# One layer with two recurrent mixers and a ConvFFN: two additions of the out-projection stage made by accumulating GpSimd transfers, and a new order of all engines

## The chip, the cores and the metric

The kernel runs on one core of a Trainium2 chip. The metric is the time on the device, in microseconds (us), of one execution, from its start to its end. A core has five engines that run side by side, each with its own queue of instructions: TensorE (PE in the profile, its weight loads PEld), VectorE (DVE), ScalarE (ACT), GpSimd (POOL) and SyncE (SP). Transfers between the core's memory and the chip's main memory are issued by SP or by GpSimd and carried out by 16 DMA engines.

## The reference

One layer, 1024 wide, works on 1152 tokens: 1024 latent tokens and 128 context tokens. Two mixers share one input projection; each runs over the tokens in both directions. Their outputs are added, normalised, projected and added to the input (the residual), and a gated feed-forward network with a 3x3 convolution follows. Cut to what matters here:

```python
h = rmsnorm(x, norm_mix_w) * (1 + scale1) + shift1
u = h @ w_in
o_a = rmsnorm(o_f + flip(o_b), hgrn_norm_w) * silu(g)          # HGRN2, chunks of 64 tokens
y = y_f + flip(y_b)                                            # RWKV-7: the two directions
yn = (y - mean(y)) * rsqrt(var(y) + GN_EPS) * ln_w + ln_b      # per head of 64
o_b = (yn + bonus) * g
x = x + gate1 * (concat([o_a, o_b]) @ w_out)                   # residual
h = rmsnorm(x, norm_ffn_w) * (1 + scale2) + shift2
gt = dwconv(h @ ffn_w_gate) + ffn_conv_b
x = x + gate2 * ((gelu(gt) * (h @ ffn_w_up)) @ ffn_w_down)
```

All is float32. The outputs are the normed x of latent and context tokens and the mixers' new states.

## The kernel before, in words

The tokens lie in nine row tiles of 128 rows: tiles 0 to 7 are latent, tile 8 is the context. A float32 matrix product is made of three float32r matmuls: each operand is split into a rounded high part and a low rest (`split`), and hi·hi, lo·hi and hi·lo are added in PSUM.

**How the order comes about.** The kernel's code issues nothing itself. It records every operation with its tiles in a `Plan`, and `schedule()` then places the operations one by one on the engines, by a model of their durations: on each engine the ready operation of the highest rank comes next. The rank is the length of the work that hangs on the operation, plus a lead from two tables: `LEADS` by the piece of code that recorded it, and `NUDGE` by the operation's number divided by 16. `BUSY` is a bonus for dense matmuls where PE has been used little in the model's last stretch. `issue()` emits the order so found, with its waits. A change of the recorded operations or of these numbers can thus move instructions anywhere on any engine. `ld` is a load issued by SP; `st` is a store that goes to POOL or SP, whichever the plan finds better; `combine` is a VectorE operation on two tensors. Where a program's name ends in a number (`wh_131`), the number is a buffer's.

**The stages.** Up to about 490 us the input is normed, modulated and projected (L1125 to L1127, three matmuls of 128x384 a step). From about 486 to 973 us the RWKV chains run in 18 steps of 64 tokens for two groups of heads, with the HGRN2 blocks, the adaLN rows (L1032 to L1038) and the rest of the projections between them. L1302 is a transpose on PE that feeds from the copy L1298. In a chain step, L1631, L1646, L1776, L1820, L1827, L1846 and L1848 are small matmuls on PE. L1767 copies values, some of them on GpSimd. L1776 reads a tile that was loaded from `d_ak`. A step's outputs are written to the array `yd` in main memory, one half of it for each direction (L1875).

As soon as the rows of a tile are complete, `wo_tile(i)` handles the out-projection of that tile, in the order 3, 4, 8, 2, 5, 1, 6, and last 0 and 7 together. Its steps:

- `post` loads both directions of y (L1915, 512 KB) and the bonus and gate rows (L1916), adds the directions (L1921, VectorE, 128x512), norms y by heads (up to L1931), and transposes it (L1935).
- 48 matmuls with the out-projection's weights follow (L2011 to L2013), and VectorE multiplies their result by the gate (L2015).
- x is loaded (L2003, 512 KB), and added as the residual (L2017, VectorE, 128x1024). The sum is stored to `x2d` (L2018), since the FFN's end needs it again.
- The root mean square is worked out (L1134 to L1137); L2019 on ScalarE normalises, L2025 transposes on PE, L1991 scales and shifts on ScalarE or VectorE, and L2034 stores the result, save for the last two tiles.

From about 1033 us on the FFN runs: L2120 multiplies by the gate and up weights, in a scheme of partial products: the "a" ones of 320 columns (operand `qm`), then the "b" ones of 256 columns (operands `ham` and `hbm`, which are made of the last tiles' result by L2057 and L2053). The down projection (L2269 to L2271) and a last norm end the kernel.

Of the kernel before, what the change touches and what calls it, by code (L numbers as in the profile page):

```python
# [18 lines left out]
MUL, ADD, SUB = ALU.mult, ALU.add, ALU.subtract  # L19
# [24 lines left out]
FETCH = 42.0  # L44
AHEAD = 240.0
HUNGRY = 2.04
BUSY = 168.59
NUDGE = {1: 6, 3: -7, 4: -41, 5: -2, 7: 9, 8: 9, 9: 9, 10: 9, 11: 20, 12: 19, 13: 19, 14: 15, 15: 15, 16: 5, 17: -4, 18: -1, 19: -4, 20: -18, 21: -29, 22: -19, 23: -26, 24: -26, 25: -6, 27: -3, 28: -3, 29: -3, 30: -3, 31: -5, 32: -3, 33: -3, 35: -3, 51: -5, 52: -5, 53: -2, 84: -6, 85: -6, 86: -6, 87: -6, 88: 6, 91: -3, 92: -6, 93: -6, 94: -6, 95: -6, 96: -6, 97: -6, 98: -6, 104: -7, 105: -4, 108: -6, 109: 4, 110: -6, 111: -6, 119: 6, 127: -7, 140: 6, 141: 6, 142: 6, 143: 21, 144: 6, 145: 6, 147: -2, 172: -17, 173: -17, 174: -17, 175: -17, 183: -14, 184: -20, 185: -4, 189: 57, 190: 57, 191: 69, 193: 5, 194: 3, 200: -15, 201: -8, 203: 11, 204: 14, 206: 3, 212: -16, 217: 13, 218: 5, 224: -48, 225: -15, 226: -15, 227: -15, 236: 7, 239: -2, 243: -26, 244: -26, 245: -26, 246: -19, 247: -26, 251: 7, 252: 7, 253: 5, 254: -12, 266: -4, 269: 3, 275: 61, 282: -16, 290: -9, 292: 2, 294: 18, 295: 18, 296: 18, 297: 28, 298: 28, 299: 28, 300: 48, 301: 48, 302: 30, 303: 27, 305: 30, 306: 30, 307: 30, 308: 37, 309: 40, 310: 40, 311: 40, 312: 51, 313: 42, 314: 47, 315: 43, 316: 23, 317: 26, 318: 26, 319: 23, 320: 23, 321: 23, 322: 23, 323: 22, 328: 10, 329: 13, 330: 29, 331: 29, 337: -10, 338: -10, 339: -10, 340: -10, 341: -10, 342: -10, 343: -10, 344: 10, 345: 10, 346: 5, 347: 8, 348: 8, 349: 8, 350: 11, 351: 8, 352: -12, 353: -14, 354: -8, 355: -14, 356: 15, 357: -2, 358: 33, 359: 7, 360: -4, 361: 4, 362: -3, 363: -4, 364: 7, 365: -7, 367: 13, 368: 23, 370: 25, 377: 6, 378: 13, 379: 13, 380: 18, 381: 18, 382: 18, 390: 1, 396: 6, 398: 5, 400: -10, 401: -10, 404: -6, 405: -6, 406: -6, 407: -6, 408: -6, 409: -6, 410: -6, 411: -6, 412: -6, 413: -2, 416: -23, 417: 3, 418: 3, 419: 3, 425: -3, 426: -3, 427: -3, 428: -3, 453: -3, 454: -3, 455: -5, 456: 20, 457: 5, 458: 20, 459: 3, 460: -15, 461: 1, 462: -4, 463: -11, 464: -4, 465: -4, 466: -4, 467: -4, 468: -4, 469: -2, 470: 32, 471: 15, 472: 15, 473: 16, 474: 1, 475: 1, 476: 15, 477: 10, 478: 14, 479: 15, 480: 28, 481: 10, 482: 12, 483: 34, 484: 24, 485: 26, 486: 6, 487: 21, 488: 6, 489: 11, 490: 20, 491: 13, 492: 25, 493: 2, 494: -16, 495: -5, 496: -5, 497: -5, 498: -5, 499: -43, 500: -20, 501: -18, 502: -16, 503: -39, 504: -13, 505: -12, 506: -12, 507: -15, 508: -36, 509: -37, 510: -24, 511: -24, 512: -38, 516: 21, 517: 22, 518: 22, 519: 11, 520: 11, 521: 11, 522: 1, 523: 11, 524: 1, 525: 11, 526: 9, 527: 26, 528: -1, 529: 1, 530: -5, 532: -34, 533: -34, 534: -26, 535: -27, 536: 8, 537: 22, 538: 22, 539: 45, 540: 16, 541: 18, 542: 14, 543: 14, 544: 4, 545: 13, 546: 4, 547: 4, 548: 53, 549: 39, 550: 39, 551: 52}
LEADS = {'ada_block': 46.4, 'bonus_rows': 27.8, 'chains': -35.7, 'const': 113.0, 'conv_rkv': 0.0, 'down_weights': -36.2, 'elim': -4.6, 'features': 0.0, 'ffn_down': 14.5, 'ffn_mid': -1.7, 'finish': 52.5, 'finish_last': -12.3, 'first_columns': -38.6, 'front': 0.0, 'gate_row': 0.0, 'hgrn_block': -3.6, 'hgrn_in': 0.0, 'hgrn_out': 113.5, 'late': -0.7, 'made': 3.5, 'mod_columns': -1.2, 'mod_scale': 70.4, 'modulated': -24.2, 'pair': 8.2, 'param_loads': 9.6, 'params': -96.8, 'post': 3.0, 'prep': 119.5, 'product': -3.4, 'put': 0.0, 'save': 4.8, 'step_kernel': -1.0, 'stored': 0.0, 'three': -10.1, 'total': -0.3, 'turned': 4.0, 'weights': 0.0, 'wo_tile': 5.1}


C_W0, C_A0, C_KK, C_KA, C_RK, C_LNW, C_LNB = 0, 8, 12, 16, 20, 24, 28
# [125 lines left out]
class Plan:  # L178


    PIECES = ("proj", "small_proj", "norm_rows", "modulate", "gate_rows", "load_step", "load_values", "conv_tiles")
    HELPERS = ("mm", "st", "copy", "combine", "split", "load_w", "record", "either")
    ENGINES = ("PE", "DVE", "ACT", "POOL", "SP")
    BITS = 23
    ROW = 1 << 16
# [94 lines left out]
    @staticmethod  # L280
    def operands(m, args, kw):

        isap = lambda x: isinstance(x, AP)
        w = [args[0]]
        r = [x for x in args[1:] if isap(x)]
        for k, x in kw.items():
            if isap(x):
                (w if k == "accum_out" else r).append(x)
        if (m == "matmul" and not kw.get("start", True)) or m == "copy_predicated":
            r.append(args[0])  # L290
        return w, r

# [526 lines left out]
def step_kernel(ctx: ExitStack, tc: tile.TileContext, I, O):  # L819
    cp = ctx.enter_context(tc.tile_pool(name="cp", bufs=1, side="left", reuse_waits="tile"))  # L820
    plan = Plan(tc, cp.tile([P, 1], F32, name="base"))
    act, dve, pool, pe = (plan.engine(e) for e in ("ACT", "DVE", "POOL", "PE"))
    ld = plan.engine("SP").dma_start

    def st(out, src):

# [1084 lines left out]
    def post(i, oh, ol, early):  # L1911

        r = slice(i * P, (i + 1) * P)
        yt, vg = (tl(t + "10"[early], [P, 2, 512]) for t in ("py", "pvg"))
        ld(yt, yd[r])  # L1915
        ld(vg, vbd[i])  # L1916
        y, sq = yt[:, 0], yt[:, 1]
        hd = heads_of
        small = tl("sm" if early else "sm1", [P, 4, 8])
        each = lambda j: view(small, 8 * j, [[1, 8], [0, 64]])  # L1920
        combine(y, y, sq, ADD)  # L1921
        dve.tensor_reduce(small[:, 0], hd(y), mybir.AxisListType.X, ADD)
        dve.tensor_scalar(small[:, 0], small[:, 0], -1.0 / 64, None, MUL)
        combine(hd(y), hd(y), each(0), ADD)
        act.activation(sq, y, AF.Square)
        dve.tensor_reduce(small[:, 1], hd(sq), mybir.AxisListType.X, ADD)
        act.activation(small[:, 2], small[:, 1], AF.Sqrt, scale=1.0 / 64, bias=eps[:, 2:3])
        dve.reciprocal(small[:, 3], small[:, 2])
        combine(hd(y), hd(y), each(3), MUL)
        combine(y, y, vg[:, 1], MUL)  # L1930
        combine(y, y, vg[:, 0], ADD)  # L1931
        ps = pbank("a")
        with plan.together():
            for p in range(NPAIR):
                pe.transpose(ps[:, p * P:(p + 1) * P], y[:, p * P:(p + 1) * P], ident)  # L1935
        split(oh[:, 4:8], ol[:, 4:8], ps.rearrange("p (k t) -> p k t", k=4))
# [58 lines left out]
    def wo_tile(i, early):  # L1995

        raw = tl("wr", [P, 4, P])
        ld(raw, odram.rearrange("k p t -> p k t")[:, :, i * P:(i + 1) * P])
        oh, ol = tl("wh", [P, KT, P], F32R), tl("wl", [P, KT, P], F32R)
        split(oh[:, 0:4], ol[:, 0:4], raw)  # L2000
        post(i, oh, ol, early)
        x, x2 = tl("xw" if early else "xr", [P, 1024]), tl("x2w" if early else "x2", [P, 1024])
        ld(x, x_src(i))  # L2003
        g1 = gate1[:, i // 8 * 1024:(i // 8 + 1) * 1024]
        for n in range(2):
            nc_ = slice(n * 512, (n + 1) * 512)
            ps = pbank()
            for kt in range(KT):
                woh, wol = wo[kt, n]
                with plan.together():  # L2010
                    mm(ps, oh[:, kt, :], woh, kt == 0, False)  # L2011
                    mm(ps, oh[:, kt, :], wol, False, False)  # L2012
                    mm(ps, ol[:, kt, :], woh, False, kt == KT - 1)  # L2013
                plan.follow("dense")
            dve.tensor_tensor(x2[:, nc_], ps, g1[:, nc_], MUL)  # L2015
            yield
        combine(x2, x2, x, ADD)  # L2017
        st(x2d[i], x2)  # L2018
        act.activation(x, x2, AF.Identity, scale=norm_rows(x2, x, "nssw" if early else "nss2"))  # L2019
        t = x2.rearrange("p (k t) -> p k t", k=KT)  # L2020
        for k0 in (0, 4):
            ps = pbank("a")
            with plan.behind(scaled), plan.together():
                for kt in range(k0, k0 + 4):
                    pe.transpose(ps[:, (kt - k0) * P:(kt - k0 + 1) * P], x[:, kt * P:(kt + 1) * P], ident)  # L2025
            for kt in range(k0, k0 + 4):
                modulate(t[:, kt, :], ps[:, (kt - k0) * P:(kt - k0 + 1) * P], kt, i // 8,
                         ("ACT", "DVE") if i in (0, 7) else ("ACT",))
        yield t
# [366 lines left out]
```

## Time and profile before

| | |
|---|---|
| median of 3 runs | 1820.85 us (1820.06 to 1825.13) |
| the profiled execution's own time | 1820.69 us |
| its span, first to last instruction | 1818.9 us |
| mean granted TensorE clock | 0.993 |
| PE busy, of the span | 97% |
| VectorE, ScalarE, GpSimd busy | 78%, 47%, 16% |

A line of the profile names the engine, the line of the code, the operation, and the tiles that it writes and reads (`out<-in`, the tile's pool, such as `low` or `top`, where no name is its own). A wait is put down to the operation that came last of those that the instruction waited for. The granted clock is TensorE's, as a share of full speed. The DMA share is the mean busy share of the 16 DMA engines.

### The profile page before, as it was taken

The numbers are of one execution on the slowest core, as the hardware profiler recorded it, in microseconds if no ns is written. First come the engines' busy times: TensorE is split into PE (matmuls) and PEld (weight loads), VectorE is DVE, ScalarE is ACT, GpSimd is POOL, SyncE is SP. The second block draws the span as 40 slices with busy tenths as digits, with TensorE's granted clock in tenths as the row PEclk, the third lists the DMA queues.
The fourth block names the chain that finished last, engine by engine and source line by source line (L and its number), as shares of the span: only waits on it lengthen the run. The fifth ranks groups of instructions, "written<-read, shape, count | busy, mean of one in ns | idle before, by whom it ended". The sixth has DMA issues, their size and how long they took to land.

```text
span 1818.9 us, 45180 instructions
## 1 busy us (share of the span) xinstructions
PE 1768.3 (97%) x18402; PEld 1587.1 (87%) x18402; DVE 1415.1 (78%) x2670; ACT 862.0 (47%) x1753; POOL 289.3 (16%) x553
## 2 busy tenths in 40 slices
PE   7999999999999999999999999999999999999998
PEld 5889888899888788888788799999999999888887
DVE  7559899887778888876867889999999954985543
ACT  6556656543255645643636754444444433321321
POOL 2013435353312222122110100000000000000000
PEclk9999999999999999999999999999999999999999
DMA  9325637487757568889967522222222247774451
GB/s 325 102 72 151 147 102 180 128 229 193 207 165 246 165 203 258 267 283 306 324 207 244 203 59 73 73 73 73 73 73 73 76 126 251 227 272 162 133 169 67
DMA packets 272176, 307.45 MB, mean 169 GB/s; under 512 B 62611, under 2 KB 216849, under 8 KB 271968
## 3 DMA queue, kind: packets, MB, share of 16 engines
q1 hardware_dynamic: 245584, 224.33, 41.3%
q0 software_dynamic: 26384, 80.23, 13.1%
q8 instruction: 144, 2.36, 0.5%
q14 instruction: 64, 0.52, 0.1%
HBM read 200.50 MB, written 103.99 MB: 167 GB/s over the span
## 4 chain that ended last, share of the span: by engine, by line
PE 69%; DMA 5%; DVE 3%; ACT 1%; issue 1%; POOL 0%; SPq 0%; DVEq 0%; ACTq 0%; POOLq 0%
PE banks L2120 27%; PE banks L2269 5%; PE banks L2270 5%; PE banks L2271 5%; PE banks L1125 3%; PE banks L1127 3%; PE banks L1126 3%; DMA low<-d_ak 2%; PE banks L2011 2%; PE banks L2013 2%; PE banks L2012 2%; PE banks L1776 1%; PE banks L1827 1%; PE banks L1846 1%; PE banks L1646 1%
## 5 line engine op out<-in xcount | busy, mean ns | idle before, releaser
L1125 PE MATMUL banks<-hh,wh 128*128 128x384 f32 x768 | 282.0, 367 | 0.7 <-DVE fx L1314 0.7
L1127 PE MATMUL banks<-hh,wl 128*128 128x384 f32 x768 | 259.0, 337 | 0.0
L1126 PE MATMUL banks<-hl,wh 128*128 128x384 f32 x768 | 258.7, 337 | 0.0
L2209 DVE SCALAR_TENSOR_TENSOR low<-low,pf 128x1024 f32<-128x1024 f32 x176 | 224.8, 1279 | 4.6 <-ACT low L2203 3.0
L2120 PE MATMUL banks<-qm,wh 128*128 128x320 f32 x968 | 223.3, 310 | 0.0
L2120 PE MATMUL banks<-hbm,wh 128*128 128x256 f32 x880 | 164.4, 283 | 1.3 <-ACT low L1991 1.3
L1125 PEld LDWEIGHTS banks<-hh,wh 128*128 128x128 f32 x768 | 144.9, 189 | 21.0 <-issue 11.4
L2120 PE MATMUL banks<-qm,wl 128*128 128x320 f32 x528 | 162.8, 308 | 0.0
L2120 PEld LDWEIGHTS banks<-qm,wh 128*128 128x128 f32 x968 | 160.7, 189 | 0.1
L1126 PEld LDWEIGHTS banks<-hl,wh 128*128 128x128 f32 x768 | 145.5, 189 | 2.4 <-issue 1.2
L1127 PEld LDWEIGHTS banks<-hh,wl 128*128 128x128 f32 x768 | 145.0, 189 | 0.0
L2120 PEld LDWEIGHTS banks<-hbm,wh 128*128 128x128 f32 x880 | 140.4, 191 | 1.7 <-ACT low L1991 1.7
L2120 PE MATMUL banks<-ham,wh 128*128 128x256 f32 (+1 forms) x616 | 132.4, 295 | 0.0
L2120 PE MATMUL banks<-hbm,wl 128*128 128x256 f32 x440 | 124.8, 284 | 0.0
L2120 PEld LDWEIGHTS banks<-ham,wh 128*128 128x128 f32 x616 | 102.2, 192 | 0.0
L2120 PEld LDWEIGHTS banks<-qm,wl 128*128 128x128 f32 x528 | 99.1, 188 | 0.0
L2269 PE MATMUL banks<-qm,hbm 128*128 128x512 f32 (+1 forms) x240 | 93.7, 390 | 0.0
L2270 PE MATMUL banks<-qm,hbm 128*128 128x512 f32 (+1 forms) x240 | 93.6, 390 | 0.0
L2271 PE MATMUL banks<-qm,hbm 128*128 128x512 f32 (+1 forms) x240 | 93.5, 390 | 0.0
L2090 ACT CAST wh<-fx 128x512 fp32r<-128x512 f32 x88 | 54.3, 620 | 80.6 <-PE banks L2120 76.0
L2158 ACT COPY fx<-banks 128x320 f32<-128x320 f32 (+1 forms) x132 | 52.0, 397 | 84.2 <-PE banks L2120 82.8
L2120 PEld LDWEIGHTS banks<-hbm,wl 128*128 128x128 f32 x440 | 84.4, 192 | 0.0
(527 smaller groups left out, 4333.5 us busy)
## 6 DMA issues: line engine op xcount, KB each, us to landing
wr<-in_w_in_dram SPq DMA_DIRECT2D x34, 512.0 KB, 5.6
d_a<-low POOLq DMA_DIRECT2D x22, 576.0 KB, 3.4
low<-d_ak SPq DMA_DIRECT2D x64, 192.0 KB, 4.4
low<-in_ffn_w_up_dram SPq DMA_DIRECT2D x22, 512.0 KB
wr<-in_ffn_w_gate_dram SPq DMA_DIRECT2D x22, 512.0 KB, 3.7
low<-d_kb SPq DMA_DIRECT2D x36, 256.0 KB, 5.3
low<-d_a SPq DMA_DIRECT2D x12, 704.0 KB, 4.6
low<-in_ada_w_dram SPq DMA_DIRECT2D x32, 256.0 KB, 6.0
```

The source lines that it names most:

```text
L1125: mm(o, wh[:, kt, :], hh[:, kt, c], kt == 0, False)
L1126: mm(o, wh[:, kt, :], hl[:, kt, c], False, False)
L1127: mm(o, wl[:, kt, :], hh[:, kt, c], False, kt == KT - 1)
L2011: mm(ps, oh[:, kt, :], woh, kt == 0, False)
L2012: mm(ps, oh[:, kt, :], wol, False, False)
L2090: split(*w, src)
L2120: pe.matmul(o, a[:, kt, :], b[:, kt, :], start=start and first, stop=last, skip_group_check=not start)
L2158: act.copy(keep[n], y[:, 0:w])
L2209: dve.scalar_tensor_tensor(av, shifted(dy, dx), tap(3 * dy + dx), av, MUL, ADD)
L2269: mm(o, lh, w[:, 0, c], first, False)
L2270: mm(o, lh, w[:, 1, c], False, False)
L2271: mm(o, ll, w[:, 0, c], False, last)
```

## The change

Two additions on VectorE become transfers that GpSimd issues and that add their data to what the destination holds (`add_from`).

- In `post`, only the first direction of y is loaded by SP. The second is then added to it on arrival. The add L1921 is gone, for all nine tiles.
- In `wo_tile`, x is loaded and added by VectorE only for tiles 0 and 7. For the seven others the transfer of x adds to the gated product that lies in `x2`. It waits for L2015, and the store of the sum, as well as the norm, wait for its landing.
- The plan takes the destination of such a transfer as read, too. The three numbers or tables that set the order are given new values, so that the order differs on every engine.

The number of PE's matmuls, 13379, stays as it was. The lines of the new code stand four lower than before up to `wo_tile` and eight lower from L2018 on: L1298 is L1302 after, L1767 is L1771, L1875 is L1879, and the store L2018 is L2026. The accumulating transfers are L1920 (y) and L2025 (residual) of the new code.

```diff
-BUSY = 168.59
-NUDGE = {1: 6, 3: -7, 4: -41, 5: -2, 7: 9, 8: 9, 9: 9, 10: 9, 11: 20, ...
-LEADS = {'ada_block': 46.4, 'bonus_rows': 27.8, 'chains': -35.7, ...
+BUSY = 185.69
+NUDGE = {1: 6, 3: -7, 5: -2, 8: 9, 9: 4, 10: 40, 11: 51, ...
+LEADS = {'ada_block': 46.4, 'bonus_rows': 35.3, 'chains': -35.7, ...
...
-        if (m == "matmul" and not kw.get("start", True)) or m == "copy_predicated":
+        if (m == "matmul" and not kw.get("start", True)) or m == "copy_predicated" or "accum_op" in kw:
             r.append(args[0])
...
+    def add_from(out, src):
+
+        plan.engine("POOL").dma_start(out, src, accum_op=ADD)
+
...
         yt, vg = (tl(t + "10"[early], [P, 2, 512]) for t in ("py", "pvg"))
-        ld(yt, yd[r])
+        ld(yt[:, 0], yd[r, 0])
+        add_from(yt[:, 0], yd[r, 1])
         ld(vg, vbd[i])
...
-        combine(y, y, sq, ADD)
...
         x, x2 = tl("xw" if early else "xr", [P, 1024]), tl("x2w" if early else "x2", [P, 1024])
-        ld(x, x_src(i))
+        if i in (0, 7):
+            ld(x, x_src(i))
...
-        combine(x2, x2, x, ADD)
+        if i in (0, 7):
+            combine(x2, x2, x, ADD)
+        else:
+            add_from(x2, x_src(i))
         st(x2d[i], x2)
```

How the order moved is shown at three places. The first is ScalarE (ACT) at about 345 us of the profiled execution, in the projection stage; L1298 is the copy on which the transposes L1302 wait, L1447 and L1448 are activations of the features. Before:

```order
L1442 ACTIVATE top<-top,eps 128x6x64
L1395 ACTIVATE top<-banks,dp 128x384
L1447 ACTIVATE top<-top 128x390
L1448 ACTIVATE top<-top 128x390
L1447 ACTIVATE top<-top 128x390
L1448 ACTIVATE top<-top 128x390
L1298 COPY fx<-banks 128x384
L1303 COPY fx<-banks 128x384
```

The same place after, with the copy as L1302 and the activations as L1451 and L1452:

```order
L1446 ACTIVATE top<-top,eps 128x6x64
L1399 ACTIVATE top<-banks,dp 128x384
L1302 COPY fx<-banks 128x384
L1451 ACTIVATE top<-top 128x390
L1402 ACTIVATE top<-top,dp 128x384
L1452 ACTIVATE top<-top 128x390
L1451 ACTIVATE top<-top 128x390
L1452 ACTIVATE top<-top 128x390
L1307 COPY fx<-banks 128x384
```

The copy has moved ahead of the four activations.

The second place is PE at about 497 us, between projection matmuls and the chains' small matmuls. Before:

```order
L1820 MATMUL banks<-low 64x64 x8
L1125 MATMUL banks<-hh,wh_131 128x384
L1126 MATMUL banks<-hl,wh_131 128x384
L1127 MATMUL banks<-hh,wl_133 128x384
L1631 MATMUL banks<-top 32x32 x24
L1646 MATMUL banks<-top 32x32 x12
L1776 MATMUL banks<-low 128x128 x8
L1827 MATMUL banks<-low 64x64 x8
```

After, where L1129 to L1131 are the projection, L1635 was L1631, L1831 was L1827 and L1780 was L1776:

```order
L1131 MATMUL banks<-hh,wl_133 128x384
L1129 MATMUL banks<-hh,wh_131 128x384
L1130 MATMUL banks<-hl,wh_131 128x384
L1131 MATMUL banks<-hh,wl_133 128x384
L1635 MATMUL banks<-top 32x32 x24
L1650 MATMUL banks<-top 32x32 x12
L1831 MATMUL banks<-low 64x64 x8
L1780 MATMUL banks<-low 128x128 x8
```

Three more projection matmuls stand ahead of the first chain matmul, and the matmuls that read the tile from `d_ak` stand behind eight others.

The third place is GpSimd from about 905 us on, where the chains' last steps and the first out-projection tiles share its queue; a DMA row is the issue of a transfer. Before:

```order
L1875 DMA d_y<-top 128x256 x4
L1038 DMA d_g_68<-top 2x128 x2
L2018 DMA d_x_117<-top 128x1024
L1767 COPY low<-low 64x256 x2
L1038 DMA d_g_68<-top 2x128 x2
L2018 DMA d_x_117<-top 128x1024
L2034 DMA d_h_118<-top 128x1024
L1767 COPY low<-low 64x256
```

After:

```order
L1920 DMA fx<-d_y 128x512
L1042 DMA d_g_68<-top 2x128 x2
L1879 DMA d_y<-top 128x256 x4
L1771 COPY low<-low 64x256 x3
L2025 DMA top<-in_x_sample_dram 128x1024
L1042 DMA d_g_68<-top 2x128 x2
L2026 DMA d_x_117<-top 128x1024
L1771 COPY low<-low 64x256
L1920 DMA fx<-d_y 128x512
L2042 DMA d_h_118<-top 128x1024
L1920 DMA fx<-d_y 128x512
L2025 DMA top<-in_x_prompt_dram 128x1024
```

Accumulating transfers now stand in the queue, and the store L2026, which waits for the landing of L2025, stands ahead of a value copy L1771 and of the next accumulating transfers.

More of the change, by code (lines that the diff above doesn't have):

```diff
@@ L49 @@
-LEADS = {'ada_block': 46.4, 'bonus_rows': 27.8, 'chains': -35.7, 'const': 113.0, 'conv_rkv': 0.0, 'down_weights': -36.2, 'elim': -4.6, 'features': 0.0, 'ffn_down': 14.5, 'ffn_mid': -1.7, 'finish': 52.5, 'finish_last': -12.3, 'first_columns': -38.6, 'front': 0.0, 'gate_row': 0.0, 'hgrn_block': -3.6, 'hgrn_in': 0.0, 'hgrn_out': 113.5, 'late': -0.7, 'made': 3.5, 'mod_columns': -1.2, 'mod_scale': 70.4, 'modulated': -24.2, 'pair': 8.2, 'param_loads': 9.6, 'params': -96.8, 'post': 3.0, 'prep': 119.5, 'product': -3.4, 'put': 0.0, 'save': 4.8, 'step_kernel': -1.0, 'stored': 0.0, 'three': -10.1, 'total': -0.3, 'turned': 4.0, 'weights': 0.0, 'wo_tile': 5.1}
+BUSY = 185.69
@@ new lines @@
+LEADS = {'ada_block': 46.4, 'bonus_rows': 35.3, 'chains': -35.7, 'const': 113.0, 'conv_rkv': 0.0, 'down_weights': -37.5, 'elim': -4.6, 'features': 0.0, 'ffn_down': 14.5, 'ffn_mid': 5.0, 'finish': 52.3, 'finish_last': -12.3, 'first_columns': -38.6, 'front': 18.7, 'gate_row': 30.3, 'hgrn_block': -3.6, 'hgrn_in': 0.0, 'hgrn_out': 113.5, 'late': -0.7, 'made': 3.5, 'mod_columns': -1.2, 'mod_scale': 70.4, 'modulated': -1.3, 'pair': 8.2, 'param_loads': 9.6, 'params': -96.8, 'post': 3.0, 'prep': 119.5, 'product': -9.6, 'put': -37.5, 'save': -17.1, 'step_kernel': 5.8, 'stored': 3.8, 'three': -6.0, 'total': -0.3, 'turned': 4.0, 'weights': 0.0, 'wo_tile': 5.1}
@@ L181 @@
     PIECES = ("proj", "small_proj", "norm_rows", "modulate", "gate_rows", "load_step", "load_values", "conv_tiles")
-    HELPERS = ("mm", "st", "copy", "combine", "split", "load_w", "record", "either")
+    HELPERS = ("add_from", "mm", "st", "copy", "combine", "split", "load_w", "record", "either")
     ENGINES = ("PE", "DVE", "ACT", "POOL", "SP")
```

2 lines of the change are left out of this document (1 added, 1 removed).

## The prediction

> **What bounds the kernel now.** I read the profile page first, then the waits of TensorE, then the time by windows, and last the timeline around the longest waits. The page says that TensorE (PE) is busy almost throughout:
>
> ```profile
> span 1818.9 us, 45180 instructions
> ...
> PE 1768.3 (97%) x18402; PEld 1587.1 (87%) x18402; DVE 1415.1 (78%) x2670; ACT 862.0 (47%) x1753; POOL 289.3 (16%) x553
> ```
>
> Only 1818.9 − 1768.3 = 50.6 us of the span have no matmul in them. The change leaves the matmuls as they are, so an order can win at most those 50.6 us, and what a lower clock costs inside the busy time. The waits of PE (engine, waiting instruction, whom it waits for: total, times, longest) show who ends that idle time. These are the rows that the change can reach:
>
> ```profile
> PE banks L2025 <- DVE fx L2057: 3.8, 1, 3.8
> ...
> PE banks L1302 <- ACT fx L1298: 2.8, 2, 2.3
> PE banks L1776 <- DMA low<-d_ak: 2.5, 6, 1.0
> ...
> PE banks L2120 <- ACT low L1991: 1.3, 1, 1.3
> ...
> PE banks L1631 <- ACT top L1617: 1.2, 2, 0.9
> PE banks L1935 <- DVE fx L1931: 1.1, 2, 1.0
> ...
> PE banks L2011 <- DVE low L2015: 0.7, 1, 0.7
> ```
>
> The reader should see that no row is large: the idle time is a sum of small stalls. The two places that the code change edits directly, the sum of the directions (L1921, behind which L1931 and L1935 come) and the residual (L2017), show 1.1 and 0.7 us.
>
> The windows give, after the stretch and its length, the busy time of PE, PEld, DVE, ACT and POOL, then the granted clock, the share of the DMA engines and GB/s:
>
> ```profile
> 345.00:348.00 3.00, 0.93 (x7) 0.93 (x8) 2.93 (x9) 2.30 (x6) 0.69 (x2) 0.99 0.00 0
> 348.00:352.00 4.00, 4.00 (x16) 4.00 (x15) 3.93 (x7) 0.13 (x1) 1.38 (x2) 0.58 0.31 80
> ```
> ```profile
> 495.00:500.00 5.00, 3.80 (x77) 2.87 (x77) 2.72 (x6) 2.91 (x6) 0.54 (x1) 1.00 1.10 243
> 500.00:505.00 5.00, 4.13 (x65) 3.46 (x68) 2.89 (x6) 1.58 (x6) 0.39 (x1) 0.66 0.55 156
> 505.00:510.00 5.00, 5.00 (x123) 4.33 (x123) 3.36 (x8) 2.44 (x6) 0.00 (x0) 0.66 0.42 132
> ...
> 1040.00:1050.00 10.00, 4.94 (x28) 4.28 (x27) 7.93 (x18) 7.89 (x17) 0.00 (x0) 0.71 0.00 1
> 1050.00:1060.00 10.00, 10.00 (x66) 10.00 (x66) 9.44 (x17) 7.27 (x16) 1.21 (x1) 0.77 0.22 63
> 1080.00:1125.00 45.00, 45.00 (x339) 45.00 (x339) 40.87 (x60) 21.29 (x39) 1.06 (x2) 1.00 0.24 77
> ```
> ```profile
> 810.00:920.00 110.00, 107.55 (x1765) 89.94 (x1764) 79.25 (x183) 51.53 (x109) 21.09 (x41) 1.00 1.02 316
> ```
>
> Two things stand here. From 1080 us on (the FFN) PE has 45.00 of 45 us: nothing that is freed elsewhere helps there. And at three places an idle stretch is followed by a lower clock: 4 × 0.42 = 1.7 us are lost after 348, 2 × 5 × 0.34 = 3.4 us from 500 to 510, and 2.9 + 2.3 = 5.2 us from 1040 to 1060. So a stall costs its length and some clock behind it.
>
> **The change, part by part.** The profiled execution took 1820.69 us, 0.16 under the median, so the sum is made against 1820.7.
>
> *The order near 345 us (ACT).* Columns: start, duration, engine and operation, and in brackets the idle time before it.
>
> ```profile
> 344.59 0.52 ACT L1447 ACTIVATE top<-top 128x390 f32<-128x390 f32 x1
> ...
> 346.56 0.46 ACT L1298 COPY fx<-banks 128x384 f32<-128x384 f32 x1
> ```
> ```profile
> 347.07 0.33 PE L1302 MATMUL banks<-c_ident,fx 128*128 128x128 f32 x1 [2.28 <-ACT fx L1298]
> ```
>
> PE waited 2.28 us for the copy L1298, which stood behind four activations. In the new order the copy stands right behind L1395, so it can start where the first of the four did, at 344.59 or, since PE had work until 347.07 − 2.28 = 344.79, just after that. It comes 346.56 − 344.79 = 1.8 us earlier: −1.8. The stall left would be 0.5 us; of the 1.7 us of clock lost behind it I take half, −0.9. The activations that the copy passes come 0.46 us later, and in the old order PE did not wait for them here.
>
> *The order near 497 us (PE).*
>
> ```profile
> 497.17 0.45 PE L1125 MATMUL banks<-hh,wh 128*128 128x384 f32 x1
> 497.45 0.34 PE L1126 MATMUL banks<-hl,wh 128*128 128x384 f32 x1
> 497.63 0.33 PE L1127 MATMUL banks<-hh,wl 128*128 128x384 f32 x1
> 498.89 0.27 PE L1631 MATMUL banks<-top 128*32 128x32 f32 x8 [0.93 <-ACT top L1617]
> ...
> 501.81 1.01 PE L1776 MATMUL banks<-low 64*128 64x128 f32 x6 [0.59 <-DMA low<-d_ak]
> ```
>
> Three more projection matmuls (at the spacing of 0.17 to 0.28 us that the first rows show, about 0.5 us) now stand ahead of L1631: −0.5 of its 0.93. L1776, which waited 0.59 for a load, now stands behind the eight L1827: −0.6. Of the 3.4 us of clock I take 1.0, since half of the idle time there stays.
>
> *The last two tiles (0 and 7), where the chains meet the FFN.* They keep the add on VectorE; only the order changes.
>
> ```profile
> 1039.94 0.15 DVE L1137 RECIPROCAL low<-low 128x1 f32<-128x1 f32 x1
> ```
> ```profile
> 1043.38 1.15 ACT L1991 ACTIVATE low<-banks,modc,modA 128x128 f32<-128x128 f32 x3 [0.54 <-DVE low L1991]
> 1044.42 1.15 ACT L2019 ACTIVATE low<-low 128x1024 f32<-128x1024 f32 x1
> 1045.61 0.62 ACT L2053 CAST hbm<-fx 128x512 fp32r<-128x512 f32 x1
> ```
> ```profile
> 1033.57 0.39 PE L2013 MATMUL banks<-wom,wl 128*128 128x512 f32 x1
> ...
> 1041.56 0.31 PE L2120 MATMUL banks<-qm,wl 128*128 128x320 f32 x1
> 1045.62 1.97 PE L2025 MATMUL banks<-c_ident,low 128*128 128x128 f32 x8 [3.75 <-DVE fx L2057]
> 1048.90 0.80 PE L2120 MATMUL banks<-hbm,wh 128*128 128x256 f32 x2 [1.31 <-ACT low L1991]
> ```
>
> The second tile's scale was ready at 1040.09, yet its normalisation L2019 began at 1044.42, behind the first tile's modulations L1991. The transposes L2025 began as it ended, so the releaser named in the row is not the true one. In the new order both normalisations stand together and all sixteen transposes follow the last "a" product. They would start near 1041, and the chain then ends in the modulations: about nine on ACT at 1.15/3 = 0.38 us with four casts L2053 of 0.62 between, 5.9 us, so the first "b" product starts near 1047.3 in place of 1048.9: −1.6. That is half of what the normalisation gains; the rest turns into waiting for modulations. I take no clock back here, because some 3 to 4 us of idle time stay.
>
> *Work taken off VectorE.*
>
> ```profile
> L1921 DVE TENSOR_TENSOR fx<-fx x7: 673/685/694, 856.1 to 995.6; 128x512 f32<-128x512 f32 x7
> ```
> ```profile
> L2017 DVE TENSOR_TENSOR low<-low x6: 1215/1220/1224, 980.8 to 1034.7; 128x1024 f32<-128x1024 f32 x6
> ```
>
> Nine adds at 0.685 and seven at 1.22 us go: 14.7 us of DVE, all between 856 and 1035 us. PE hides them: what it waited for there is the 1.1 and 0.7 us above. Of this 1.8 I take 0.5.
>
> *The accumulating transfers.* Sixteen are added, nine of 256 KB and seven of 512 KB; nine loads shrink by 256 KB and seven of 512 KB go. None of before's transfers accumulates, so the price is bounded by the nearest plain ones, the loads L1916 and the stores L2018 (first the issue on GpSimd in ns, then issue to landing):
>
> ```profile
> DMA to landing us min/median/max: 5.6/5.9/8.0
> ```
> ```profile
> L2018 POOL DMA_DIRECT2D d_x<-low x5: 531/533/537, 982.3 to 1036.2; - x5
> ...
> DMA to landing us min/median/max: 2.9/4.0/8.3
> ```
> ```profile
> L1767 POOL COPY low<-low 64x256 f32<-64x256 f32 x13 | 6.0, 464 | 44.6 <-DMA low<-d_v 33.4 <-PE banks L1835 8.0 <-PE banks L1776 3.1
> ```
>
> On GpSimd sixteen issues of 0.53 us are 8.5 us, which its idle time hides (21.09 of 110 us busy from 810 to 920). What matters is the waiting. Each y accumulate waits for the load of the first direction (about 5.9 us), and the store behind a residual accumulate waits for its landing; behind these stand the value copies L1767 of the scan and the stores of chunk outputs. From below, those copies already wait 33.4 us for loads over the window, so a hold may cost nothing; a gain is excluded, as nothing is taken off this queue. From above it is the first rival's 15 us. I take +1.0, near the low end, because PE's stalls in this window are 110.00 − 107.55 = 2.45 us and the copies have waited for loads all along.
>
> The landing is also on the path of the tile: load and accumulate in a row take 11.8 us where the load took 5.9. By my reading of the new order, the last y accumulate and the residual of tile 6 are issued 9 to 10 us before their result is needed; a landing up to 8.3 us fits.
>
> The Trainium skill ("DMA: Bandwidth & Descriptors", section "Rules for kernel authors") says that an accumulate reads its destination and writes it later. By that rule each moves more bytes than a copy of its size, and with the price of the fourth rival the sum would be 1818.1 in place of 1814.8; by the rows above it stays, and no run of before can show which.
>
> *The rest of the order.* It is set anew on every engine. At the three places that I followed, the stall became shorter each time; elsewhere I know no sign and take 0, from −10 to +10 (a fifth of the 50.6 us either way).
>
> Sum: −1.8 −0.9 −0.5 −0.6 −1.0 −1.6 −0.5 +1.0 = −5.9, so 1820.7 − 5.9 = 1814.8 us.
>
> **The rivals.** *First, slower: GpSimd's queue is held by the accumulations.* If an accumulate lands in twice the longest store (2 × 8.3 = 16.6 us), the last y accumulate and the residual of tile 6 are each 7 to 8 us later than PE needs them: +15. It decides from a landing of some 9 us on. For it: two waits for a landing now stand in a row on a queue that also feeds the scan. Against it: GpSimd is busy 16%, and the plain landings are under 8.3 us. Time: 1814.8 + 15 = 1829.8. Chance 0.22.
>
> *Second, no change: the stalls move.* Each gain shortens one of many small stalls, and the next instruction in line may wait instead. The rows above speak for it: five different releasers share the time. Half to all of the 6.9 us of gains is given back, the +1.0 stays: 1818 to 1822, 1819 taken. Chance 0.14.
>
> *Third, a larger gain: the new order shortens the stalls all along.* If a third of the 50.6 us goes, that is 17: 1804. For it: three of three places got better. Against it: the stalls of the chains follow data dependences that stay. Chance 0.16.
>
> *Fourth, traffic.* From 810 to 920 us the DMA engines are busy without a gap (share 1.02 at 316 GB/s). If each y accumulate moves its 256 KB once more, as it would if it read its destination first, the four tiles there add 1.05 MB, 3.3 us at that rate, and if PE waits for all of it the time is 1814.8 + 3.3 = 1818. Against it: PE's waits of L1776 for its loads are 2.5 us in the whole run. Chance 0.03.
>
> **How the numbers follow.** The forecast, 1814.8, has the chance that is left, 0.45, with its own range of 1810 to 1818. About 0.3% (5.5 us) is what a measurement of this kernel tells from no change: faster is under 1815.4, slower over 1826.3. Of the forecast 0.40 counts as faster and 0.05 as the same. Faster: 0.40 + 0.16 = 0.56. Same: 0.05 + 0.14 + 0.03 = 0.22. Slower: 0.22. The range goes from 1802, a little beyond the third rival, to 1830, the middle of the first; it leaves out the upper half of that one (0.11) and the lower part of the third (0.06).
>
> **What would show it.** Right: the stall before L1302 near 345 us at 0.5 us and the clock behind it near 1; the two small stalls near 500 us gone; the first "b" product about 13.3 us after the last product of the out-projection (14.9 now: 1048.9 less the end of L2013, 1034.0); PE's idle time at 45 us or below; accumulations landing within 8.3 us. Wrong: a landing over 9 us with L1935 or L2025 waiting for a transfer (first rival), the same total idle time under other lines (second), or PE's waits for d_ak and d_v grown between 810 and 920 us (fourth).

## The result and the profile after

Measured beside each other, the changed kernel takes 1835.30 us (median, 1834.87 to 1842.18) and the kernel before 1820.45 us (1820.05 to 1825.13). The ratio is 1.0084, with a 95% interval of 1.0056 to 1.0113: slower by about 15 us. The forecast was 1814.8 us and faster, with a range that ended at 1830. The execution that was profiled has a span of 1833.1 us.

The page of the changed kernel, the lines that answer to those shown before (busy time, share of the span, instructions):

```profile
span 1833.1 us, 45116 instructions
...
PE 1772.0 (97%) x18402; PEld 1586.0 (87%) x18402; DVE 1405.6 (77%) x2669; ACT 858.6 (47%) x1743; POOL 302.7 (17%) x567
```

VectorE has lost 9.5 us of work and PE has gained nothing: its idle time (span less busy time) grew from 50.6 to 61.1 us and its busy time by 3.7 us. The number of PE's matmul records is 18402 in both. The waits of PE in the changed kernel, without the two largest rows (L1199 and L1005), which belong to the start of the kernel and stand in both (10.5 us here, 11.4 before):

```profile
PE banks L2033 <- ACT low L1995: 3.6, 2, 1.9
PE banks L1839 <- DVE low L1858: 2.7, 1, 2.7
PE banks L1306 <- ACT fx L1302: 2.3, 4, 0.6
PE banks L1780 <- DMA low<-d_ak: 2.1, 3, 1.5
PE banks L2033 <- ACT low L2027: 2.1, 2, 1.9
...
PE banks L1530 <- DVE top L1515: 1.5, 1, 1.5
PE banks L1036 <- DMA fx<-in_ada_w_dram: 1.4, 1, 1.4
```

Again many small stalls, but partly others. L1530 (features) is new in the list. L1839 (scan, L1835 before) waits 2.7 us for the VectorE operation L1858, in place of 0.7 us. The transposes L2033 (L2025 before) wait 5.7 us in these two rows, in place of 3.8.

The accumulating transfers, first those of y (the row has seven of the nine), then the residual ones (four of the seven): issue time on GpSimd as lowest, median and highest ns; who waited for the landing; issue to landing, which the trace has for six of the nine and four of the seven:

```profile
L1920 POOL DMA_DIRECT2D fx<-d_y x7: 860/881/923, 854.2 to 1011.0; - x7
...
DMA to landing us min/median/max: 4.1/6.2/9.5
```
```profile
L2025 POOL DMA_DIRECT2D low<-in_x_sample_dram x4: 854/874/884, 985.3 to 1025.4; - x4
...
  ACT low L1138: 7.9, 4
  ACT top L1138: 6.9, 2
...
DMA to landing us min/median/max: 5.5/7.5/8.2
```

The first transfer is issued at 854 us. The residual ones land within the 8.3 us that the prediction allowed, and so do the y ones but one, which took 9.5. Yet ScalarE stands 14.8 us before L1138, the square sum of the norm, waiting for them.

To see where the time goes although the order differs, I weighed each PE instruction with the usual distance to the next one for its line in the trace of before, and compared when the same sum of work is done. This is called the comparison of work below. By this reading of the two traces the changed kernel is 5.0 us ahead at 350 us of the kernel before, 5.6 ahead at 725, then 2.7 behind at 850, 9.6 at 925, 10.4 at 1000 and 14.8 at 1075; from there to the end, in the FFN, nothing changes (14.1 at 1800). So some 8 us are lost before the first accumulating transfer exists, and 12 after it.

One caution comes from the experiments below. Six of them issue the same instructions in the same order up to that first transfer, and their profiled executions stand between 3.7 us ahead and 6.7 behind at 850 us. A single trace is thus good to some 5 us before 850; the medians and ratios decide.

### The profile page after: what moved, and what is told of

It is laid out like the page before. It is cut to its first block, busy times and chain, and to the rows that moved or that the text cites. A ratio compares the mean times of both kernels' runs of the same rounds, so it can differ in the third digit from the quotient of the medians.

```text
span 1833.1 us, 45116 instructions
## 1 busy us (share of the span) xinstructions
PE 1772.0 (97%) x18402; PEld 1586.0 (87%) x18402; DVE 1405.6 (77%) x2669; ACT 858.6 (47%) x1743; POOL 302.7 (17%) x567
## 5 line engine op out<-in xcount | busy, mean ns | idle before, releaser
L1129 PE MATMUL banks<-hh,wh 128*128 128x384 f32 x768 | 281.9, 367 | 0.4 <-DVE fx L1318 0.4
L1131 PE MATMUL banks<-hh,wl 128*128 128x384 f32 x768 | 258.7, 337 | 0.1
L1129 PEld LDWEIGHTS banks<-hh,wh 128*128 128x128 f32 x768 | 145.0, 189 | 20.5 <-issue 11.3
L1131 PEld LDWEIGHTS banks<-hh,wl 128*128 128x128 f32 x768 | 145.0, 189 | 0.0
L2277 PE MATMUL banks<-qm,hbm 128*128 128x512 f32 (+1 forms) x221 | 86.4, 391 | 0.0
L2278 PE MATMUL banks<-qm,hbm 128*128 128x512 f32 (+1 forms) x221 | 86.3, 391 | 0.0
L2279 PE MATMUL banks<-qm,hbm 128*128 128x512 f32 (+1 forms) x221 | 86.3, 390 | 0.0
```

The source lines that it names most:

```text
L1129: mm(o, wh[:, kt, :], hh[:, kt, c], kt == 0, False)
L1131: mm(o, wl[:, kt, :], hh[:, kt, c], False, kt == KT - 1)
L2277: mm(o, lh, w[:, 0, c], first, False)
L2278: mm(o, lh, w[:, 1, c], False, False)
L2279: mm(o, ll, w[:, 0, c], False, last)
```

## The experiments

Three questions: is it the new order or the transfers; if the transfers, is it adding or the length of the wait; and where does the wait hurt? The ratios are to the kernel before, run beside each.

**The transfers in the old order.** The order of before is kept on PE, on ScalarE and, but for the adds, on VectorE. Where an add stood, a marked operation is issued as a transfer instead (a cut of the edit; its second new line leaves out the load of x):

```diff
         combine(x2, x2, x, ADD)
+        if i not in (0, 7):
+            plan.swap(whole, None)
+            plan.swap(plan.ops[-1], None, ("POOL", "dma_start", (x2, x_src(i)), dict(accum_op=ADD)))
```

and in the same way for y, whose load brings one direction and whose transfer is issued where that load was planned to have landed.

> The order of before on every engine; only the nine y adds and seven residual adds are made by accumulating GpSimd transfers. The y accumulate is issued when its first half is planned to have landed, the residual one where the add stood. Landing theory: the waits for the landings (median 6.2 and 7.5 us in the changed kernel's trace) on the ScalarE and VectorE queues cost 12 us or so: about 1832. Order theory: the new order costs the time and the transfers next to nothing: within 3 us of before, 1818 to 1823.

Measured: 1880.17 us, ratio 1.0328 (1.0297 to 1.0359). Both theories were far too low: the transfers alone cost about 60 us where nothing is moved for them. Its trace tells how; VectorE's waits from 850 to 1100 us (engine, waiting instruction, releaser: total, times, longest):

```profile
DVE low L1934 <- DMA fx<-d_y: 18.9, 3, 13.4
DVE low L1144 <- ACT low L1143: 18.8, 4, 6.0
DVE top L1144 <- ACT top L1143: 16.2, 2, 8.3
DVE top L1934 <- DMA fx<-d_y: 13.4, 2, 7.4
```

L1934 is the first reader of y, L1143 and L1144 the square sum and the scaling of the norm (1922, 1134 and 1135 before). VectorE stands still for 67 us in front of readers of landings, and everything behind them in its queue, the scan and the FFN's operands included, stands too. In the trace of before VectorE waits 2.0 us in all for the loads of y and 1.3 us for ScalarE's square sum. By the pages of the two runs, PE's idle time is 94.6 us in place of 50.6, and its busy time is 15.8 us longer at a mean granted clock of 0.980 in place of 0.993.

**The new order without the transfers.** The order of the changed kernel is kept and the sixteen transfers are not issued:

```diff
                 e, l = op.forms[0]
+                if l[0][2].get("accum_op") is not None and True:
+                    continue
```

> The order of the changed kernel, with all sixteen accumulating transfers left out (so y lacks its second direction and seven tiles their residual). Landing theory: what comes after 854 us is won back, some 12 us: about 1823. Order theory: it stays near 1833.

Measured: 1823.19 us, ratio 1.0007 (0.9989 to 1.0025). The landing theory's number. The new order by itself, with all the adds gone, is worth nothing that can be measured, neither gain nor loss; the transfers cost 1.0084 − 1.0007, about 14 us (8 to 20 by the two intervals).

**Writing instead of adding.** The same order and the same transfers, with `accum_op` left away when they are issued.

> The order of the changed kernel; the sixteen transfers write instead of adding (so y is the second direction alone, x2 the old x). If adding is what makes the landing long: the median landing of the y transfers falls from 6.2 to about 4 us, of the residual's from 7.5 to about 5, and the time by 3 to 6 us, to about 1831. If any GpSimd transfer of this size at this place takes as long: the landings and 1835 stay.

Measured: 1825.14 us, ratio 1.0021 (0.9999 to 1.0043). Some 11 us came back (5 to 18 by the two intervals), where 3 to 6 were expected. The y transfers, then the residual ones (here the trace has the landing of four y and two residual transfers):

```profile
L1920 POOL DMA_DIRECT2D fx<-d_y x7: 541/546/558, 847.7 to 998.4; - x7
...
DMA to landing us min/median/max: 4.6/5.4/6.9
```
```profile
L2025 POOL DMA_DIRECT2D low<-in_x_sample_dram x4: 532/532/535, 973.5 to 1012.0; - x4
...
  ACT low L1138: 2.5, 1
  ACT top L1138: 0.6, 1
DMA to landing us min/median/max: 3.9/4.0/4.2
```

The residual lands after 4.0 us in place of 7.5, and ScalarE's wait shrinks from 14.8 to 3.1 us. So in the new order most of the price lies in adding; what mere transfers cost there is not told from nothing.

How large is it by the traces? From 850 to 1075 us, where the drift of the earlier part drops out, the comparison of work gives a loss of 12 us for the changed kernel, 4.2 without the transfers and 4.1 with writing ones. That is some 8 us for the transfers by single traces, at the low end of what the ratios give.

**The same in the old order.**

> The order of before with the sixteen transfers in it, but they write instead of adding (y is the second direction alone, x2 the old x). Landings were 5.4 and 4.0 us for writing, 6.2 and 7.5 for adding, in the changed kernel's order. If the cost goes by the length of the wait, about two thirds of the 57 us stay (9.4 of 13.7 us a tile): 1850 to 1865. If adding itself disturbs other work: 1835 or less.

Measured: 1853.62 us, ratio 1.0189 (1.0167 to 1.0211). As expected of the length of the wait: some 34 us are left of about 60, so in this order even plain transfers are dear. Its waits on VectorE in the same stretch:

```profile
DVE low L1934 <- DMA fx<-d_y: 16.0, 3, 11.4
DVE low L1144 <- ACT low L1143: 11.3, 4, 3.9
DVE top L1934 <- DMA fx<-d_y: 10.0, 2, 6.6
DVE top L1144 <- ACT top L1143: 7.8, 2, 5.8
```

They add up to 45 us in place of 67. Time and waits fall together.

**The residual alone in the old order.**

> The order of before with the seven residual transfers alone; y is added on VectorE. If the residual is the dearer half, as its longer landing says: 1850 to 1860. If the two share the 57 us by number (9 to 7): about 1845.

Measured: 1855.97 us, ratio 1.0188 (1.0165 to 1.0212): the seven residual transfers alone cost some 34 of the 60 us, as expected if the residual is the dearer half. The y transfers alone were not run in this order.

**One half left out in the new order.** As the second experiment, but only the seven residual transfers, or only the nine of y, are not issued.

> The order of the changed kernel without the seven residual transfers (seven tiles lack their residual); the nine y accumulates stay. If the residual's landing (7.5 us, on which ScalarE waits 14.8 us in all) carries the cost: about 1825. If y's: about 1833.

Measured: 1829.48 us, ratio 1.0036 (1.0015 to 1.0056).

> The order of the changed kernel without the nine y transfers (y lacks its second direction); the seven residual transfers stay. If the residual's landing carries the cost: about 1833. If y's: about 1825.

Measured: 1830.65 us, ratio 1.0042 (1.0023 to 1.0062). Neither expectation: in the new order each half alone costs about as much as the other, some 7 us over the kernel before.

**The readers put later, old order.** The planned time of what reads a transfer's result is moved on, through all that depends on it, and the operations are sorted again under all their dependences, so that other work goes ahead of the waiting reader (a cut of the edit; the two times are those of the y and the residual transfers):

```diff
+                op.end = op.start + 7.0
+            elif forms:
+                op.end = op.start + (8.4 if forms[0][1][0][2] else 3.0)
         self.order = sorted(ops, key=lambda o: (o.start, o.id))
+        self.retime(0.0)
```

> The accumulating transfers in the order of before (1880 us), with the same move: the transfers are given 7.0 us (y) and 8.4 us (residual) from issue to landing in the planned times, and what reads them is sorted later. Queue theory: the greater part of the 57 us comes back, 1825 to 1840. Chain theory: 1870 or more.

Measured: 1846.20 us, ratio 1.0133 (1.0104 to 1.0162). It lies between the two ranges, nearer to that of the queue theory. More than half of the cost comes back, with the same transfers and landings that are no shorter (medians of the few that the trace has: 6.4 and 8.4 us, against 5.8 and 7.0 before the move), by moving a few dozen rows on VectorE and ScalarE and some transposes on PE. In the old order the queues behind the waiting readers are thus the greater part of the mechanism. What is left stands mostly before the readers of y (6 waits from 850 to 1100 us, 29.5 us in all), which this move did not clear:

```profile
DVE low L1986 <- DMA fx<-d_y: 20.8, 4, 7.7
DVE top L1986 <- DMA fx<-d_y: 8.7, 2, 7.3
```

**The readers put later, new order.** There the mechanism can be seen in full at two places. ScalarE, VectorE and PE of the changed kernel around 932 us (start, duration, instruction, idle time before it and its releaser):

```profile
931.78 1.06 ACT L1138 ACTIVATE top<-top 128x1024 f32<-128x1024 f32 x1 [3.01 <-DMA top<-in_x_sample_dram]
```
```profile
932.97 0.15 DVE L1139 TENSOR_SCALAR top<-top 128x1 f32<-128x1 f32 x1 [2.43 <-ACT top L1138]
933.15 0.43 DVE L1858 TENSOR_TENSOR low<-banks,dcs 64x256 f32<-64x256 f32 x1
```
```profile
933.63 0.48 PE L1839 MATMUL banks<-low 128*64 128x64 f32 x4 [2.72 <-DVE low L1858]
```

The norm of tile 3 waits for its residual; the scan's L1858 stands behind the norm's L1139, though it needs nothing of it; PE's scan matmuls wait for L1858, and the granted clock of the window from 930 to 940 us is 0.83. The second place is at 1020 us:

```profile
1018.01 0.69 DVE L1926 TENSOR_REDUCE low<-fx 128x8 f32<-128x512 f32 x1 [3.25 <-DMA fx<-d_y]
```
```profile
1019.76 0.15 DVE L1139 TENSOR_SCALAR low<-low 128x1 f32<-128x1 f32 x1
```
```profile
1023.20 1.09 PE L2033 MATMUL banks<-c_ident,low 128*128 128x128 f32 x8 [1.90 <-ACT low L2027]
```

Here the norm of one tile (L1139, whose square sum was ready at about 1016 us) stands on VectorE behind the first reader of another tile's y, and PE waits 1.90 us for the transposes that come of that norm. In the order without the transfers PE has neither stall. Two kernels move such readers:

> The changed kernel, with one thing moved: what reads the result of an accumulating transfer is put 3.5 us later in the planned times (about what the landings measured over the planner's figure), and the order is sorted again under all dependences, so that other ready work on VectorE and ScalarE goes ahead of it. Some 75 rows of VectorE's order and 40 of ScalarE's change. Queue theory (the scan's and the FFN's work stands behind norms that wait for a landing): some 8 of the 12 us come back, about 1826. Chain theory (the tile's own path is too long, whatever stands behind it): 1833 to 1838.

Measured: 1842.26 us, ratio 1.0100 (1.0066 to 1.0133).

> The changed kernel, with only the readers of the seven residual transfers sorted 4 us later (the y chains stay where they are). The stall of 2.7 us at 934 us, where the scan's work stood behind a norm that waited for a landing, should go by the queue theory, and with it the lower clock behind it: 1828 to 1831. Chain theory: the stall comes back within the stage, 1833 to 1840.

Measured: 1836.48 us, ratio 1.0087 (1.0066 to 1.0109). No gain in either, as the chain theory had it, the first even above its range. In the second, the stall of 2.72 us at 934 us is gone, but PE stops soon after for the transposes of y (L1988), and at 1020 us for those of the residual's norm (L2082, which was L2033):

```profile
935.24 0.66 PE L1988 MATMUL banks<-c_ident,fx 128*128 128x128 f32 x4 [1.37 <-DVE fx L1984]
```
```profile
1020.13 1.19 PE L2082 MATMUL banks<-c_ident,low 128*128 128x128 f32 x8 [2.06 <-ACT low L2076]
```

A reader that steps back in VectorE's queue is late for PE's own queue, in which these transposes stand where they stood. So these two shifts win nothing in the new order. How its 14 us divide between queues, as at 932 and 1020 us, and the tiles' own chains stays open: the two runs fit the chain theory, but no run shortened a chain alone.

**Tables and code apart.** The tables of the changed kernel with the code of before, and the reverse. The planner then makes yet other orders, so these say what the tables are worth, not what one place costs.

> The code of before (all adds on VectorE) with the three tables of the changed kernel; the planner makes an order of its own from them. The changed order without its transfers measured 1.0007 of before. If the tables hold a gain that the transfers hide: 1805 to 1815. If not: 1820 to 1830. If the tables only fit the changed code: 1835 or more.

Measured: 1844.31 us, ratio 1.0129 (1.0107 to 1.0151): the tables fit only the code that they were set for. Most of the loss is one wait of PE, at the start of the FFN:

```profile
PE banks L2120 <- ACT qm L2053: 13.7, 1, 13.7
```

> The changed code with the three tables of before (the planner still makes a new order for the new operations). Landing theory: 1830 or more. Order theory, the new tables at fault: 1819 to 1824.

Measured: 1889.66 us, ratio 1.0379 (1.0347 to 1.0411), near the transfers in the old order. The new tables are what brings the changed code from 69 us over the kernel before down to 15.

No run pointed to a version that beats the kernel before: with the transfers left out altogether the new order only equals it.

## Why the prediction was wrong

**What failed first: the price of the accumulating transfers.** The sum had +1.0 for them; the runs show about +14 (1.0084 against 1.0007). The length of the landing was the smaller mistake: the medians of 6.2 and 7.5 us and all landings that the trace has but one, of 9.5, lie below the 8.3 us that the plain rows gave. The mistake was where the wait was looked for. The prediction named what stands behind it on GpSimd's queue and asked of the tile's path only whether the last y and the residual of tile 6 come in time. It did not ask what stands behind the first readers on VectorE and ScalarE, L1926, L1138 and L1139, for each of the sixteen. Even for the two it named, the first readers stood ready sooner than the 9 to 10 us after the issue that it read from the order. L1926 waited 3.25 us for the last y (above; issued at 1010.96), and ScalarE waited for the residual of tile 6, which was issued at 1025.43 and landed after 5.5 us:

```profile
1031.00 1.06 ACT L1138 ACTIVATE low<-low 128x1024 f32<-128x1024 f32 x1 [1.17 <-DMA low<-in_x_sample_dram]
```

So they stood ready 3.8 and 4.4 us after the issue. The VectorE add that was removed was short (0.69 and 1.22 us) and ran when the product was there; its replacement holds the two queues of its readers for what is left of the landing. That this is the greater part of the cost is shown for the old order, where putting the readers later brought more than half of it back. In the new order the cost as a whole is shown, and the two places above; how the rest divides is open.

GpSimd's queue, which the first rival accused, was no place of loss. From 850 to 1100 us no wait of PE, VectorE or ScalarE is put down to GpSimd, and its copies waited for their loads nearly as before:

```profile
POOL low L1771 <- DMA low<-d_v: 78.1, 20, 18.6
```

That is 78.1 us over the run, where the trace of before has 75.2 for L1767.

The first rival thus came within 5.5 us of the measured time (1829.8 against 1835.3) by luck, with the wrong mechanism. It was to decide from a landing of some 9 us on; the residual never took more than 8.2, y's median was 6.2, and the one y transfer of 9.5 us held VectorE for 2.4 us before L1926, not GpSimd's copies.

**What failed second: the order.** The forecast counted −6.9 us for it, clock and VectorE relief included. The new order without the transfers measured 1.0007, that is +1.3 us, between −2 and +5. Two of its three places came true and gave more than was counted: by the comparison of work the changed kernel gains 4.3 us from 344 to 356 us and 4.5 us from 494 to 512, where 2.7 and 2.1 were forecast.

```profile
342.93 0.55 PE L1306 MATMUL banks<-c_ident,fx 128*128 128x128 f32 x3 [0.57 <-ACT fx L1302]
```
```profile
348.00:352.00 4.00, 3.42 (x65) 2.48 (x64) 3.86 (x10) 3.63 (x7) 2.20 (x4) 1.00 0.74 184
...
460.00:470.00 10.00, 8.51 (x73) 7.87 (x72) 9.31 (x22) 2.54 (x5) 1.12 (x3) 0.96 0.36 106
470.00:480.00 10.00, 10.00 (x110) 9.66 (x110) 4.38 (x7) 1.61 (x2) 5.44 (x10) 0.87 0.68 194
...
500.00:505.00 5.00, 4.55 (x112) 3.63 (x107) 3.81 (x9) 2.40 (x6) 0.39 (x1) 1.00 1.05 264
505.00:510.00 5.00, 4.87 (x145) 4.08 (x141) 4.27 (x12) 2.86 (x8) 0.00 (x0) 1.00 0.48 130
720.00:730.00 10.00, 8.27 (x131) 7.44 (x120) 5.44 (x12) 3.08 (x8) 2.00 (x4) 0.83 0.97 314
840.00:850.00 10.00, 9.97 (x105) 8.70 (x95) 3.94 (x10) 2.00 (x5) 0.29 (x1) 0.83 0.88 258
930.00:940.00 10.00, 7.28 (x98) 6.43 (x94) 3.82 (x9) 4.26 (x8) 0.95 (x2) 0.83 0.89 231
```

The stall before the transposes L1306 (L1302 before) is 0.57 us, as worked out, and the clock stays at 1.00 there and from 500 to 510 us. Near 500 us the stall of L1635 (L1631 before) is gone and that of L1780 (L1776 before) is 0.37 us in place of 0.59. But the clock falls in five windows where it was 1.00 before: about 460 and 470 us, where L1530 waited 1.5 us; at 720, where L1780 waited 1.5 us for its load from `d_ak`; at 840, where L1036 waited 1.4 us for adaLN weights; and at 930, with the norm. Behind the last two tiles it still falls, to 0.68 from 1060 to 1070 us. Over the whole execution the mean granted clock is 0.994, where it was 0.993: what the clock gave back at two places it lost at others. That is the second rival, stalls that move. The step that failed is the term "the rest of the order", which the sum put at 0: with the two places won and the order still only equal to before, it cost some 9 us (an estimate from the +1.3 us and the comparison of work of the order without the transfers: 4.2 and 5.4 us won at the two places, 1.5 lost at the last two tiles). The prediction's own bounds for it were −10 to +10. It gave the second rival 0.14 on its own and took three places for a sign of the whole; they were three that I had looked up because they stalled before.

**The last two tiles.** The sixteen transposes were to run one after the other, and the first "b" product to come 13.3 us after the out-projection. The changed kernel's PE:

```profile
1046.26 0.39 PE L2018 MATMUL banks<-wom,wl 128*128 128x512 f32 x1
...
1057.37 0.66 PE L2033 MATMUL banks<-c_ident,low 128*128 128x128 f32 x4 [1.65 <-ACT low L1995]
1059.95 1.11 PE L2033 MATMUL banks<-c_ident,low 128*128 128x128 f32 x4 [1.93 <-ACT low L1995]
1060.72 0.56 PE L2128 MATMUL banks<-ham,wh 128*128 128x256 f32 x1
1063.29 0.58 PE L2128 MATMUL banks<-ham,wh 128*128 128x256 f32 x1 [2.01 <-DVE ham L2061]
```

The second eight transposes wait twice for the modulations L1995 of the first eight; the working had all sixteen run on from 1041 us and asked for no such wait. The first "b" product comes 14.1 us after the last matmul of the out-projection, and the second one stands 2.01 us later still, so that in place of −1.6 the term is about +1. The order without the transfers shows the same: by the comparison of work it loses 1.5 us between 1000 and 1075 us.

**The other terms.** VectorE's relief was put at −0.5; with all sixteen adds gone and no transfer in their place the new order only equals the kernel before, so no gain of it can be seen. Of the 1.8 us from which it was taken, 0.7 us was the wait of L2011 for the gate product L2015, which the change leaves as it is. The FFN, put at nothing, kept its length to 0.7 us by the comparison of work done. The traffic rival is not supported by its own sign: from 810 to 920 us PE does not wait for `d_ak` or `d_v` at all, where it waited 1.4 us for `d_ak` and `d_akp` before, and the DMA share there is 0.98 (1.02 before). GpSimd's wait for `d_v` grew from 18.8 to 26.3 us in that stretch, but no wait of PE there is put down to GpSimd. The writing run does not test this rival, since it takes any extra traffic away together with the adding.

## What to carry to other kernels

When a short operation becomes a transfer, list its readers and, for each, what stands behind it on the reader's own engine: in-order queues turn a landing of 7 us into a stop for work that has nothing to do with it, while the queue that issues the transfer may not suffer at all. An order that is tuned to the microsecond and an operation's duration belong together; judge the operation in the old order and the new order without the operation, since the pair alone shows neither. And three stalls that are seen to get shorter are no sample of an order in which all stalls were dealt anew.

## What the runs showed of the hardware

In one and the same order, adding on arrival took 0.87 us to issue against 0.53 for writing, and 7.5 against 4.0 us to land for 512 KB, 6.2 against 5.4 for 256 KB. In the order of before it was 7.0 against 5.1 and 5.8 against 3.8. I had bounded it by plain transfers and not thought of a difference of this size. The medians of the landings rest on two to six transfers each. The pages of the two kernels show the same bytes on GpSimd's queue, with more packets and time; first adding, then writing:

```profile
q0 software_dynamic: 28896, 86.80, 14.9%
```
```profile
q0 software_dynamic: 28320, 86.80, 14.2%
```

Reading the destination does not appear in the bytes. The packet records of these two traces show where the time goes. The residual transfers go in packets of 4096 bytes in both, which take 0.33 us adding and 0.16 us writing (medians). The y transfers go in 128 packets of 2048 bytes, 0.18 us each, where the writing ones have 64 of 4096; nine times 64 are the 576 packets of difference. The Trainium skill ("DMA: Bandwidth & Descriptors", section "Rules for kernel authors") says that the accumulate reads its destination and writes it later; the doubled time of a packet agrees with that, and the runs do not show the reading by itself.
